# Encoder trunk on one core: weight parts kept in a DRAM scratch after their first split

## The chip, the cores and the metric

One NeuronCore of one Trainium2 chip runs the kernel; the other cores are idle. The metric is device time in microseconds (us) of one execution, as the median of several runs. Five engines matter here: PE (TensorE, matrix products), DVE (VectorE), ACT (ScalarE), POOL (GpSimd) and SP (SyncE), which computes nothing and issues every DMA of this kernel in the order of its own queue. An instruction waits on its engine until what it needs is there, and everything behind it on the same engine waits with it.

## The reference, cut to what matters

One layer and a final norm are applied to a prompt of 256 tokens and to a sample of 2048 tokens, with the same weights, all in float32:

```python
h = rms_norm(x, norm_mix_g)
proj = h @ w_in                       # 1024 x 1792: q, k, v, x_br, y_br
...
attn = bidir_gqa(apply_axial_rope(q, tables), apply_axial_rope(k, tables), v)
rec = recurrent_group(x_br, y_br, conv_w, conv_b, lru_wa, lru_ba, lru_wx, lru_bx, lru_lambda)
x = x + jnp.concatenate([attn, rec], axis=-1) @ w_out      # 1024 x 1024
h = rms_norm(x, norm_mlp_g)
x = x + jnp.square(jax.nn.relu(h @ w_up)) @ w_down         # 1024 x 4096, 4096 x 1024
return rms_norm(x, norm_final_g)
```

## The kernel before

Activations lie feature-major: 128 features on the partitions, up to 512 tokens (`NT`) on the free axis. TensorE multiplies a rounded form of float32 (float32r), so every operand is split into a high part (the value rounded) and a low part (the value minus the high part), and each product takes three matrix instructions: high weights by high tokens (L185), high weights by low tokens (L186), low weights by high tokens (L187). An instruction here takes a 128x128 weight block and 256 or 512 tokens.

The weights come as half tiles of 128x512, four 128x128 blocks each, and `WStream` (L128 to L169) streams them. For half tile i it loads the float32 values into a buffer `wf` (L145), writes the high part to a buffer `wh` by a cast (L160), and the low part to a buffer `wl` by a subtraction (L163). There are three buffers of each kind (`WBUFS`). When half tile `now` comes into use, `advance(now)` emits what is missing of the loads up to `now + 3` and of the casts and subtractions up to `now + 2` (`AHEAD = [4, 3, 3]`). The buffer of `wh` or `wl` for half tile i is that of half tile i - 3, so it comes free only when PE has done with i - 3; the buffer of `wf` comes free when the subtraction of i - 3 is done. In phase 1 cast and subtraction run on DVE. In phase 2 the cast runs on ACT; the subtraction runs on DVE, except in the prompt's block, where two of three run on POOL (`gtt`).

Phase 1 is the input projection `w_in`, in 28 half tiles. The list of half tiles names each of them three times: for the prompt (256 tokens), for the first half of the sample (two tiles of 512 tokens) and for the second half. Each time it is loaded and split again. Beside the projections run coroutines, one step at each tick of the projection stream: norms, gelu, query and key norms with rotation (`do_qk`), the recurrent group's gates and scans (`lru_sample`), and the prompt's attention. Most of their work is on DVE, and their results go to DRAM through SP.

Phase 2 goes through five blocks of tokens: the prompt's block p (256 tokens), then s0 to s3 (512 tokens each). `mlp` runs the output projection (16 half tiles), then up and down projections in groups (`up_down`, 64 and 64 half tiles), so 144 half tiles in a block and 720 in all, and all five blocks load and split all 144. At a block's start `load_cat` loads four operands of 1 MB each. The sample's attention is interleaved as a coroutine: its units for block s0 run during block p, those for s1 during s0, and so on, so s3 has none beside it. During block p the backward scans of the recurrent group (`lru_back`) run too, with their loads from DRAM. The last block's last eight half tiles are used twice and have memory of their own (`ws.kept`).

The order in each engine's queue is not the order of the program text. A planner that simulates the kernel sets it, with the text's order as priority; so a load can stand in SP's queue as soon as the planner sees its buffer free, ahead of where the text has it.

Of the kernel before, what the change touches and what calls it, by code (L numbers as in the profile page):

```python
# [19 lines left out]
P = 128  # L20
# [8 lines left out]
G = 4  # L29
# [14 lines left out]
# columns of the packed per-feature vectors  # L44
# [11 lines left out]
class Ticks:  # L56
    """Coroutines that emit a step of their work at each tick of the tensor engine's main stream."""
# [19 lines left out]
def trunk(ctx, tc, xT, w_in, w_out, w_up, w_down, vecs, wa, wx, cos, sin, outT):  # L77
# [11 lines left out]
    def loadr(out, src):  # L89
        """loads parts that were split before"""  # L90
        load(f32(out), src)
# [25 lines left out]
    # scratch in DRAM  # L117
# [10 lines left out]
    class WStream:  # L128
        """A sequence of half weight tiles (four stationaries each), loaded and split ahead of use."""

        def __init__(self, pool, srcs, ahead, bufs, copy, sub):
            self.pool, self.srcs, self.ahead, self.copy, self.sub = pool, srcs, ahead, copy, sub
            self.bufs = dict(zip(("wf", "wh", "wl"), bufs))
            self.at = [0, 0, 0]
            self.f, self.h, self.l = {}, {}, {}
            self.kept = {}  # memory for those that are used twice
# [4 lines left out]
        def load(self, end):  # L141
            while self.at[0] < end:
                i = self.at[0]
                self.f[i] = self._tile("wf", F32, i)
                load(self.f[i], self.srcs[i])  # L145
                self.at[0] += 1

        def advance(self, now):
            """emits what is due when half tile `now` comes into use"""
            self.load(min(now + self.ahead[0], len(self.srcs)))  # L150
            for st, a in list(enumerate(self.ahead))[1:]:
                while self.at[st] < min(now + a, len(self.srcs)):
                    i = self.at[st]
                    if i in self.kept:
                        tile_ = self.kept[i][st - 1]
                    else:
                        tile_ = self._tile(("wh", "wl")[st - 1], FR, i)
                    if st == 1:
                        self.h[i] = tile_
                        self.copy(i)(self.h[i], self.f[i])  # L160
                    else:
                        self.l[i] = tile_
                        self.sub(i)(self.l[i], self.f.pop(i), f32(self.h[i]), op=ALU.subtract)  # L163
# [7 lines left out]
    def faster(g, every):  # L171
        """a coroutine with one more step each time that `every` ticks have passed"""
# [16 lines left out]
    def rsqrt_newton(ps, r, w, mul):  # L189
        """r = -2 / sqrt(ps + eps), ps a mean square in PSUM"""  # L190
# [5 lines left out]
    # chunks of w_in in the order of use, for the prompt and for two halves of the sample; then all others by blocks  # L196
    order_p = [6, 7, 8, 9, 10, 11, 12, 13, 0, 1, 2, 3, 4, 5]
    order_s, order_t = ORDER_S, ORDER_T
    srcs = [h for m in order_p + order_s + order_t for h in halves(w_in[m])]
    n1 = len(srcs)  # L200
    for _ in segs:
        for m in range(0, KC, 2):
            srcs += [w_out[m][:, 0:512], w_out[m + 1][:, 0:512], w_out[m][:, 512:1024], w_out[m + 1][:, 512:1024]]
        for step in up_down():
            if step[0] == "u":
                srcs += halves(w_up[step[1] * G + step[2]])
            else:
                srcs += halves(w_down[step[1], step[2]])
    nb = (len(srcs) - n1) // len(segs)
    wp = ctx.enter_context(tc.tile_pool(name="w", bufs=1))  # L210
    ws = WStream(wp, srcs, AHEAD, WBUFS, lambda i: nc.vector.tensor_copy if i < n1 else nc.scalar.copy,
# [15 lines left out]
    right = ctx.enter_context(ExitStack())  # pools on the other side of the memory  # L227
# [5 lines left out]
    def load_cat(r, t0, n, up):  # L233
        """the output projection's operands of block r"""
# [8 lines left out]
    # ------------------------------------------------------------------ phase 1  # L243
    with ExitStack() as c1:
# [23 lines left out]
        def norm1(xs, n):  # L268
            """normalizes a token tile in place, but for the gains; then norm1_split applies them and splits"""
# [50 lines left out]
        sets = [0, 1]  # free ones of the two that hold a normalized token tile  # L320

        # the prompt's tile first
# [11 lines left out]
        CUT = 1022  # the sample's LRU segments: the first half's projections give this many outputs  # L334
        cuts = [(0, NT), (NT, CUT - NT)] + [(CUT + 342 * i, 342) for i in range(3)]

        # LRU constants: per-channel decay rates -8 softplus(-lam)
# [9 lines left out]
        # log1p(e) = 2 atanh(z), z = e/(2+e) <= 1/3  # L347
# [13 lines left out]
        # gate biases, halved for the tanh form of the sigmoid  # L361
        hba = ctile([P, 16], "hba")
        ts(hba, vec[:, V_BA:V_BA + 16], 0.5, None, op0=ALU.mult)
        # query and key gains; the -1/2 of the inverse root and the queries' 1/8 folded in
# [4 lines left out]
        # final gains with the -1/2 of the inverse root folded in  # L369
        ts(gfin, vec[:, V_GFIN:V_GFIN + 8], -0.5, None, op0=ALU.mult)  # L370

        # block-diagonal gate weights of one 128-channel chunk
# [13 lines left out]
        def project(i, h, n):  # L386
            """chunk i of the order for one token tile"""
# [22 lines left out]
        def do_qk(q, g, n, m, pos, outs):  # L410
            """head-wise norm and rotation of n columns of queries or keys, in pieces of m positions"""
# [63 lines left out]
        def lru_gates(gates, xb, xc, gt, o, m, c):  # L475
            """convolution and the tanh forms of the four gates for one piece; xb holds 2 tokens before, 1 after"""
# [20 lines left out]
        convs = {}  # pieces of each generation of xb whose convolution is still to come  # L497

        def lru(pieces, groups, w, done, gen):
            """coefficients of both directions and the forward states.  # L500
            pieces: (xb, offset, length, chunk); groups: (offset, length, chunk, carry or None)
            sigmoid = (tanh + 1)/2; a = exp(rate r); sqrt(1 - a^2) = (1 + a) sqrt(tanh(-rate r / 2))"""
# [45 lines left out]
        def lru_sample(c, xb, hf, gen):  # L548
            """one chunk for one half of the sample"""
# [12 lines left out]
        def lru_out(pool, dst, ge, ab, ub, hf, init):  # L562
            """backward states in place of ub, then the gated sum, split and stored"""
# [682 lines left out]
```

## Time and profile before

| | us |
|---|---|
| median of 3 runs | 3244.76 |
| lowest and highest run | 3243.56, 3248.42 |
| span of the profiled execution, first to last instruction | 3244.3 |
| PE busy in the span | 3014.7 (93%) |
| DVE busy | 2572.9 (79%) |
| ACT busy | 1714.2 (53%) |
| POOL busy | 1610.5 (50%) |
| DMA engines, mean busy share | 37% |

PE is the busiest engine, but the mean hides stages that have different limits, so the profile is read by stage. By the trace, the prompt's projections end near 150 us, the sample's projections near 570 us, block p near 1145 us, s0 near 1760 us, s1 near 2330 us, s2 near 2810 us, and s3 ends the span. PE's busy time counts matmuls that overlap in the pipeline once.

### The profile page before, as it was taken

What the parts mean: (1) busy time and instruction counts of PE and PEld (TensorE: products, weight loads), DVE (VectorE), ACT (ScalarE), POOL (GpSimd) and SP (SyncE); (2) the same over time, 40 slices, a digit from 0 to 9 for tenths busy, and PEclk for the clock granted to TensorE, in tenths of its full rate; (3) what the DMA queues carried; (4) which work ended last, traced back from release to release, by engine and by line L of the source; (5) the groups of instructions that cost most, each with busy time, mean ns of one, the idle gap of its engine ahead of it and who ended that gap; (6) DMA issues with size and microseconds to landing.
All of it is one profiled execution on the core that took longest, in us unless ns stands there. A gap on an engine that the chain in (4) does not pass through costs nothing.

```text
span 3244.3 us, 41376 instructions
## 1 busy us (share of the span) xinstructions
PE 3014.7 (93%) x13646; PEld 2425.1 (75%) x13646; DVE 2572.9 (79%) x3242; ACT 1714.2 (53%) x2954; POOL 1610.5 (50%) x1116
## 2 busy tenths in 40 slices
PE   6699899777898999999999999999999999999998
PEld 5576677556787778888887788888777888778887
DVE  8989988699999898887889988888898644464446
ACT  5475567555666566555555555555466333343333
POOL 4436634587899864453558444444664211321104
PEclk8899999798999999999999999999999999999999
DMA  5335344876333432222234322222442233552333
GB/s 159 116 119 194 113 148 156 223 217 189 114 98 100 153 122 74 72 73 75 77 102 150 120 76 70 81 75 71 142 148 72 89 94 95 167 164 95 94 95 104
DMA packets 222582, 380.78 MB, mean 117 GB/s; under 512 B 30752, under 2 KB 59680, under 8 KB 222368
## 3 DMA queue, kind: packets, MB, share of 16 engines
q1 hardware_dynamic: 222368, 378.15, 36.8%
q8 instruction: 107, 1.75, 0.2%
q14 instruction: 107, 0.88, 0.1%
HBM read 308.84 MB, written 69.21 MB: 117 GB/s over the span
## 4 chain that ended last, share of the span: by engine, by line
PE 60%; DVE 8%; issue 2%; DMA 2%; POOL 1%; ACT 1%; DVEq 0%; SPq 0%; POOLq 0%; ACTq 0%
PE ps_d L186 7%; PE ps_d L185 7%; PE ps_u L187 7%; PE ps_u L186 7%; PE ps_d L187 7%; PE ps_u L185 7%; PE po L940 3%; PE s_mx L839 3%; PE po L939 3%; PE s_t L936 3%; PE s_t L935 3%; DVE pl L947 2%; DVE mx L840 1%; DVE wl L163 1%; PE ps_o L185 1%
## 5 line engine op out<-in xcount | busy, mean ns | idle before, releaser
L951 POOL TENSOR_TENSOR acc<-acc,pf 128x512 f32<-128x512 f32 x448 | 692.2, 1545 | 395.6 <-ACT pf L943 359.6
L160 ACT CAST wh<-wf 128x512 fp32r<-128x512 f32 x712 | 439.7, 618 | 809.2 <-PE ps_d L186 361.4
L163 DVE TENSOR_TENSOR wl<-wf,wh 128x512 fp32r<-128x512 f32 x700 | 612.1, 875 | 211.0 <-ACT wh L160 205.6
L947 DVE TENSOR_TENSOR pl<-pf,ph 128x512 fp32r<-128x512 f32 x512 | 612.2, 1206 | 51.5 <-ACT ph L945 48.1
L187 PE MATMUL ps_u<-h2h,wl 128*128 128x512 f32 (+1 forms) x1280 | 478.8, 375 | 3.2 <-DVE wl L163 3.1
L186 PE MATMUL ps_u<-h2l,wh 128*128 128x512 f32 (+1 forms) x1280 | 478.6, 374 | 1.3 <-DVE h2l L977 1.3
L185 PE MATMUL ps_u<-h2h,wh 128*128 128x512 f32 (+1 forms) x1280 | 478.1, 374 | 0.0
L995 POOL TENSOR_TENSOR rl<-rl 128x512 f32<-128x512 f32 (+1 forms) x160 | 180.9, 1131 | 587.5 <-ACT uh L994 578.0
L185 PE MATMUL ps_d<-uh,wh 128*128 128x512 f32 (+1 forms) x1248 | 463.2, 373 | 4.1 <-ACT wh L160 3.5
L187 PE MATMUL ps_d<-uh,wl 128*128 128x512 f32 (+1 forms) x1248 | 462.5, 373 | 3.4 <-POOL wl L163 2.1
L186 PE MATMUL ps_d<-ul,wh 128*128 128x512 f32 (+1 forms) x1248 | 463.5, 373 | 2.2 <-DVE ul L997 2.2
L943 ACT ACTIVATE pf<-s_t 128x512 f32<-128x512 f32 x512 | 301.0, 594 | 225.6 <-PE s_t L936 120.9
L840 DVE TENSOR_REDUCE mx<-s_mx 128x1 f32<-128x512 f32 x512 | 344.9, 680 | 56.1 <-PE s_mx L839 55.0
L945 ACT ACTIVATE ph<-pf 128x512 fp32r<-128x512 f32 x512 | 316.9, 631 | 11.9 <-PE po L939 3.4
L187 PEld LDWEIGHTS ps_u<-h2h,wl 128*128 128x128 f32 x1280 | 243.0, 190 | 53.2 <-DVE wl L163 4.3
L186 PEld LDWEIGHTS ps_u<-h2l,wh 128*128 128x128 f32 x1280 | 243.2, 190 | 51.9 <-DVE h2l L977 2.1
L185 PEld LDWEIGHTS ps_u<-h2h,wh 128*128 128x128 f32 x1280 | 243.4, 190 | 50.7 <-issue 0.5
L185 PEld LDWEIGHTS ps_d<-uh,wh 128*128 128x128 f32 x1248 | 236.2, 189 | 53.5 <-ACT wh L160 4.9
L1108 DVE TENSOR_TENSOR y<-y,ps_d 128x512 f32<-128x512 f32 (+1 forms) x272 | 169.7, 625 | 133.5 <-PE ps_d L187 133.2
L187 PEld LDWEIGHTS ps_d<-uh,wl 128*128 128x128 f32 x1248 | 236.1, 190 | 51.8 <-POOL wl L163 2.6
L186 PEld LDWEIGHTS ps_d<-ul,wh 128*128 128x128 f32 x1248 | 236.3, 189 | 51.4 <-DVE ul L997 3.9
L185 PE MATMUL ps_in<-hh,wh 128*128 128x512 f32 (+1 forms) x560 | 221.5, 398 | 37.6 <-DVE wh L160 8.5
(277 smaller groups left out, 5823.6 us busy)
## 6 DMA issues: line engine op xcount, KB each, us to landing
wf<-in_w_up_dram SPq DMA_DIRECT2D x320, 256.0 KB, 2.7
wf<-in_w_down_dram SPq DMA_DIRECT2D x320, 256.0 KB, 2.7
wf<-in_w_in_dram SPq DMA_DIRECT2D x84, 256.0 KB, 2.9
wf<-in_w_out_dram SPq DMA_DIRECT2D x80, 256.0 KB, 2.9
x<-in_xT_dram SPq DMA_DIRECT2D x32, 256.0 KB, 5.1
qd<-q_ds SPq DMA_DIRECT2D x64, 128.0 KB, 3.0
cat<-a_ds SPq DMA_DIRECT2D x8, 1024.0 KB, 7.4
cat<-r_ds SPq DMA_DIRECT2D x8, 1024.0 KB, 9.7
```

Of the source, the lines that this page charges most:

```text
L160: self.copy(i)(self.h[i], self.f[i])
L163: self.sub(i)(self.l[i], self.f.pop(i), f32(self.h[i]), op=ALU.subtract)
L185: mm(ps, wh, xh, start=first, stop=False)
L186: mm(ps, wh, xl, start=False, stop=False)
L187: mm(ps, wl, xh, start=False, stop=last)
L840: nc.vector.tensor_reduce(mx[:, i, b:b + 1], s[:, :w], axis=AX.X, op=ALU.max)
L943: act(pf, s, AF.Exp)
L945: act(ph, pf, AF.Copy)
L947: tt(pl, pf, f32(ph), op=ALU.subtract)
L951: gtt(acc, acc, pf, op=ALU.add)
L995: gtt(e[:, :n], e[:, :n], e[:, :n], op=ALU.mult)
L1108: tt(y[:, :n], y[:, :n], ps[:, :n], op=ALU.add)
```

## The change

The list of half tiles becomes a list of keys that name which piece of which weight each one is. The first time that a key occurs, the low part gets a DRAM scratch of 128x512, and for `w_in` the high part gets one too. At the first use load, cast and subtraction are as before, and each new part is stored to its scratch by a DMA on SP's queue. At a later use of a `w_in` half tile, nothing is loaded into `wf`, and both parts are loaded from the scratch into `wh` and `wl`. At a later use of a half tile of `w_out`, `w_up` or `w_down`, the float32 values are loaded and cast by ACT as before, and the low part is loaded from the scratch in place of the subtraction. Buffer counts and distances (`WBUFS`, `AHEAD`) stay. Lines that only lose a comment are left out:

```diff
-        def __init__(self, pool, srcs, ahead, bufs, copy, sub):
+        def __init__(self, pool, srcs, saved, ahead, bufs, copy, sub):
             self.pool, self.srcs, self.ahead, self.copy, self.sub = pool, srcs, ahead, copy, sub
+            self.saved = saved
...
                 i = self.at[0]
-                self.f[i] = self._tile("wf", F32, i)
-                load(self.f[i], self.srcs[i])
+                hi, _, first = self.saved[i]
+                if first or hi is None:
+                    self.f[i] = self._tile("wf", F32, i)
+                    load(self.f[i], self.srcs[i])
                 self.at[0] += 1
...
                         tile_ = self._tile(("wh", "wl")[st - 1], FR, i)
+                    hi, lo, first = self.saved[i]
                     if st == 1:
                         self.h[i] = tile_
-                        self.copy(i)(self.h[i], self.f[i])
+                        if i in self.f:
+                            self.copy(i)(tile_, self.f[i])
+                            if first and hi is not None:
+                                store(hi, f32(tile_))
+                        else:
+                            loadr(tile_, hi)
                     else:
                         self.l[i] = tile_
-                        self.sub(i)(self.l[i], self.f.pop(i), f32(self.h[i]), op=ALU.subtract)
+                        f = self.f.pop(i, None)
+                        if first:
+                            self.sub(i)(tile_, f, f32(self.h[i]), op=ALU.subtract)
+                            store(lo, f32(tile_))
+                        else:
+                            loadr(tile_, lo)
...
-    srcs = [h for m in order_p + order_s + order_t for h in halves(w_in[m])]
-    n1 = len(srcs)
+    keys = [("i", m, e) for m in order_p + order_s + order_t for e in range(2)]
+    n1 = len(keys)
     for _ in segs:
         for m in range(0, KC, 2):
...
+            keys += [("o", m + e, b) for b in range(2) for e in range(2)]
+        keys += [(step, e) for step in up_down() for e in range(2)]
+    srcs, saved, scratch = [], [], {}
+    for key in keys:
...
+        srcs.append(halves(w)[e])
+        first = key not in scratch
+        if first:
+            scratch[key] = [dtile([P, 512], f"w{t}_d{len(scratch)}") if t == "l" or key[0] == "i" else None
+                            for t in ("h", "l")]
+        saved.append((*scratch[key], first))
```

## Rows read from the trace of the kernel before

**Rows 1.** Busy time (instructions) by engine, granted clock, DMA share in chosen stretches.

```profile
core 0: us, PE busy (x) PEld busy (x) DVE busy (x) ACT busy (x) POOL busy (x), PEclk, DMA share, GB/s
0.00:150.00 150.00, 98.00 (x508) 80.77 (x508) 140.22 (x238) 75.85 (x143) 70.33 (x55) 0.86 0.42 130
150.00:562.00 412.00, 374.34 (x1551) 291.63 (x1552) 361.55 (x471) 259.66 (x384) 195.81 (x122) 0.95 0.45 150
562.00:1145.00 583.00, 488.25 (x2715) 409.36 (x2714) 543.41 (x620) 339.95 (x636) 478.25 (x331) 0.93 0.52 155
1145.00:1240.00 95.00, 89.67 (x377) 69.28 (x376) 90.46 (x107) 59.91 (x106) 59.04 (x39) 1.00 0.34 109
1240.00:1760.00 520.00, 517.87 (x2237) 416.55 (x2237) 438.50 (x538) 292.78 (x506) 269.08 (x182) 1.00 0.27 87
1760.00:1840.00 80.00, 74.39 (x312) 57.00 (x311) 79.20 (x93) 48.18 (x83) 50.87 (x33) 1.00 0.41 136
2330.00:2410.00 80.00, 70.40 (x284) 54.18 (x283) 73.90 (x76) 45.08 (x77) 59.99 (x37) 0.96 0.50 159
2800.00:2880.00 80.00, 72.90 (x296) 55.94 (x295) 52.84 (x60) 31.02 (x52) 39.05 (x27) 0.98 0.66 211
2880.00:3180.00 300.00, 300.00 (x1287) 241.74 (x1286) 122.70 (x185) 101.82 (x171) 39.72 (x35) 1.00 0.30 96
```

**Rows 2.** Instruction groups of the split: whole span, then 150 to 562 us.

```profile
L163 DVE TENSOR_TENSOR wl<-wf,wh 128x512 fp32r<-128x512 f32 x700 | 612.1, 875 | 211.0 <-ACT wh L160 205.6
...
L163 DVE TENSOR_TENSOR wl<-wf,wh 128x512 fp32r<-128x512 f32 x50 | 43.2, 867 | 1.2
L160 DVE CAST wh<-wf 128x512 fp32r<-128x512 f32 x49 | 39.8, 815 | 0.2
```

**Rows 3.** Waits, 150 to 562 us: engine, waited for, total us, times, longest us.

```profile
POOL qk L436 <- DVE qsw L435: 52.4, 13, 11.0
...
PEld ps_in L187 <- DVE wl L163: 9.8, 8, 2.1
...
PEld ps_in L185 <- ACT qk L179: 8.5, 3, 7.3
...
PEld ps_in L185 <- DVE wh L160: 7.0, 5, 2.5
```

**Rows 4.** Timeline of PE, 2810 to 2870 us: the instructions that waited, idle before in brackets.

```profile
2824.14 0.50 PE L185 MATMUL ps_o<-cat,wh 128*128 128x512 f32 x1 [3.47 <-DMA cat<-r_ds]
2850.80 0.50 PE L187 MATMUL ps_o<-cat,wl 128*128 128x512 f32 x1 [1.36 <-DVE wl L163]
```

**Rows 5.** DMA view (count, KB, us to landing): 150-562, 562-650 (two lines), 650-820, 2900-3150 us.

```profile
wf<-in_w_in_dram SPq DMA_DIRECT2D x48, 256.0 KB, 3.0
...
q1 hardware_dynamic: 10501, 18.58, 78.3%
wf<-in_w_out_dram SPq DMA_DIRECT2D x13, 256.0 KB, 5.9
...
wf<-in_w_up_dram SPq DMA_DIRECT2D x22, 256.0 KB, 4.6
...
wf<-in_w_up_dram SPq DMA_DIRECT2D x48, 256.0 KB, 2.6
```

**Rows 6.** Timeline near 3000 us: casts of three half tiles that follow each other.

```profile
2999.67 0.62 ACT L160 CAST wh<-wf 128x512 fp32r<-128x512 f32 x1 [2.18 <-PE ps_d L186]
...
3002.47 0.62 ACT L160 CAST wh<-wf 128x512 fp32r<-128x512 f32 x1 [2.18 <-PE ps_d L186]
```

**Rows 7.** Waits of SP's queue, 150 to 562 us: total us, times, longest.

```profile
SPq L145 <- DVE wl L163: 105.3, 34, 11.7
SPq L430 <- DVE qk L434: 27.3, 16, 10.8
SPq L451 <- ACT qh L448: 22.8, 12, 6.4
```

**Rows 8.** Timeline of SP near 343 us: start, time on SP, one load.

```profile
342.75 0.33 SPq L145 DMA_DIRECT2D wf<-in_w_in_dram  x1
```

More of the change, by code (lines that the diff above doesn't have):

```diff
@@ L198, in trunk @@
     order_s, order_t = ORDER_S, ORDER_T
-    srcs = [h for m in order_p + order_s + order_t for h in halves(w_in[m])]
-    n1 = len(srcs)
+    keys = [("i", m, e) for m in order_p + order_s + order_t for e in range(2)]
+    n1 = len(keys)
     for _ in segs:
         for m in range(0, KC, 2):
[L203 to L208, printed above, removed]
+            keys += [("o", m + e, b) for b in range(2) for e in range(2)]
+        keys += [(step, e) for step in up_down() for e in range(2)]
+    srcs, saved, scratch = [], [], {}
+    for key in keys:
+        if key[0] == "i":
+            w, e = w_in[key[1]], key[2]
+        elif key[0] == "o":
+            w, e = w_out[key[1]], key[2]
+        else:
+            (kind, g, f), e = key
+            w = w_up[g * G + f] if kind == "u" else w_down[g, f]
+        srcs.append(halves(w)[e])
[4 more added lines that the diff above has]
+        saved.append((*scratch[key], first))
     nb = (len(srcs) - n1) // len(segs)
     wp = ctx.enter_context(tc.tile_pool(name="w", bufs=1))
-    ws = WStream(wp, srcs, AHEAD, WBUFS, lambda i: nc.vector.tensor_copy if i < n1 else nc.scalar.copy,
+    ws = WStream(wp, srcs, saved, AHEAD, WBUFS, lambda i: nc.vector.tensor_copy if i < n1 else nc.scalar.copy,
                  lambda i: gtt if n1 <= i < n1 + nb and i % POOL_SUB else tt)
```

## The prediction

> **What bounds the kernel now.** I read the page's busy times first, then the same by stage, then who waits for whom inside the stages where TensorE has gaps, and last the DMA landings and SP's queue. The reader is to see in the stage table that the kernel has no single limit [rows 1]. In the long stretches of blocks s0 to s3 PE is busy 517.9 of 520 us and 300.0 of 300; two more such stretches, 1840 to 2330 and 2410 to 2800 us, look alike. There PE is the bound and nothing that DVE gives up can shorten them. PE's gaps lie elsewhere: 52 us in the prompt's part (0 to 150), 37.7 us in the sample's projections (150 to 562), 95 us in block p, and 5.3, 5.6, 9.6 and 7.1 us, together 27.6 us, in four short stretches around the starts of s0 to s3. DVE is busy 93% of the prompt's part, 88% of the sample's projections, 93% of block p, and 95%, 99% and 92% at the starts of s0, s1 and s2. So DVE stands in the way in front of PE just where PE has gaps; but two of those places, the prompt's part and block p, are first uses, which the change leaves on DVE.
>
> **What is removed.** Of the 84 half tiles of `w_in`, 56 are later uses: each drops a cast of 0.815 us and a subtraction of 0.867 us, 56 x 1.682 = 94 us of DVE, of which the rows show 83 us inside 150 to 562 us [rows 2]. DVE there would go from 361.6 to some 279 us of 412, from 88% to 68%. In phase 2, 4 x 144 = 576 subtractions go, about 500 us of DVE by the mean of 875 ns [rows 2]. Of these, nearly all lie in stretches where PE has no gap, and I cost them at nothing gained: the cover is PE itself, and it cannot go.
>
> **Gain in the sample's projections.** PE's weight loads wait there 9.8 us for the low part and 7.0 us for the high part on DVE, 16.8 us, and 8.5 us for an evacuation by ACT [rows 3]; ACT's and POOL's own queues stand behind DVE, as the 52.4 us of POOL waiting for one DVE step of the rotation show [rows 3]. I take the 16.8 us whole, since these instructions no longer exist, and half of the evacuations' 8.5: 21 us. The bounds are 0 (another wait ends last in the same place) and all 37.7.
>
> **What takes the place of the wait there.** Both parts now come by DMA into `wh` and `wl`, whose buffers come free only when PE has finished the half tile three before. Before, the DMA went into `wf` ahead of that point, and only cast and subtraction lay behind it. For the second half tile of each chunk the buffer comes free one half tile before the chunk's end and the part is wanted one half tile into the next chunk: two half-tile times. One takes 2.80 us (two casts in a row, each released by PE [rows 6]), so the lead is 5.6 us. A `wf` load lands 3.0 us after its issue in this stage [rows 5]. The change adds 56 transfers of 256 KB here (112 loads for 56), 14.7 MB to some 62 MB (150 GB/s over 412 us [rows 1]), so the DMA share goes from 0.45 to about 0.56. Landings grow with the share in the rows: 2.6 us at 0.30, 3.0 at 0.45, 5.9 at 0.78 [rows 1, 5]; between these I take 3.8. That leaves 1.8 us, less 0.33 us of SP for each issue [rows 8]. On the other side stands SP's order: the queue also holds loads and stores that wait for DVE and ACT, and the two longest entries are 50.1 us in 28 waits, 1.8 us each and up to 10.8 [rows 7]. A weight load behind such a wait is late by what the slack doesn't cover, and PE waits for it. There are 28 such half tiles. The low end is 0, the high end all 28 by 1.8 us, 50 us. I take 8 us, about one in six, nearer to the low end since the mean wait just equals the slack and since the waits on SP are mostly for DVE, which gets lighter. Net for this stage: -13 us.
>
> **The prompt's part and block p: stores added.** The 28 first uses of `w_in` add 56 stores, 18 us of SP's time over 150 us at 0.33 us each [rows 1, 8], and the next `wf` load stands behind a store that waits for its subtraction. The loads have a buffer to spare; I take +1 us, between 0 and 4. Block p adds 144 stores. In its first 88 us (562 to 650) the DMA engines are already 78.3% busy and 13 output-projection loads take 5.9 us to land [rows 5]. The 17 half tiles of that time store 4.5 MB beside 18.6: share 78.3% x 23.1 / 18.6 = 97%. The extra 19% of 88 us is 17 us of DMA time; if it all delays the loads, that is the cost, and if the gaps swallow it, 0. PE and DVE both have gaps there, so I take the middle, +8. Later in block p a load lands in 4.6 us [rows 5], while 583 us for 144 half tiles is 4.0 us each and a `wf` buffer is free about three half tiles ahead; the stores hide behind DVE, which is the bound. If that cover goes, loads wait for stores, ACT's queue (the exponentials) waits behind the cast, and DVE starves; I carry that in the range.
>
> **The starts of s0 to s3.** Of PE's 27.6 us some 7 are waits for the 1 MB operands, 3.47 us at s3's start [rows 4], which no subtraction causes (the subtraction's own wait there is 1.36 us). Of the rest I take half, -10 us, since DVE is full at three of the four starts [rows 1] and the subtraction is one of its steady loads; the bounds are 0 and 20. Against it, at each start a low-part load is issued behind 2 MB of operands that are wanted at the same time, and then two 256 KB loads per half tile run beside the rest. I take +1 us at each start, +4; at most +16 if four half tiles of each are late by 1 us.
>
> **The long stretches.** A low-part load has its buffer when PE leaves half tile i - 3, so a lead of 5.6 us or more, against 2.6 us to land at a share of 0.30 [rows 1, 5, 6]. The share would go to about 0.6 in s3, the landing to about 4. Cost 0, with some 1.5 us to spare; if SP holds the load for longer, see the second rival.
>
> **The sum.** -21 + 8 + 1 + 8 - 10 + 4 = -10 us. The profiled span is 3244.3 us, half a microsecond under the median, so nothing is scaled: 3244.8 - 10 = 3235 us.
>
> **First rival: a larger gain.** The freed DVE time empties all queues behind it, no load is late, and block p's stores fit: -37.7 + 1 - 20 = -57 us, 3188 us; with half of that in place of my smaller shares, 3215. For it: the 52.4 us of POOL behind DVE [rows 3]. Against it: DMA waits take part of the same gaps. Chance 0.15, over the stretch below 3215.
>
> **Second rival: slower, late weights behind SP.** The mechanism is SP's order: one queue in which a load now waits for PE and for everything ahead of it, in place of a load that ran ahead. It decides from the point where SP holds a load longer than the slack, 1.8 us in the projections. Price: 50 us there, 17 in block p, 16 at the starts, less the gains of 31, plus 1: +53 us, 3298 us; at half of those costs, +11, 3256. I place its middle at 3272. For it: landings of 5.9 us under load [rows 5] and SP waits up to 10.8 us [rows 7]. Against it: the lead is twice the landing in quiet stretches. The Trainium skill's page "DMA: Bandwidth & Descriptors", section "Latency and other measured facts", speaks for this rival: it gives the access latency of HBM as 0.2 us on average and 2 us at high load. By that figure a load in the projections lands at an estimated 4.8 us, the slack falls to 0.8, and the sum would be about +10, 3255 us. The trace agrees in direction, with 2.6 us in the quiet stretch and 5.9 in the busy one. Chance 0.25.
>
> **Third rival: no change.** The gaps of PE stay because DMA waits end where DVE waits ended, each about as long: 3245 us. For it: PE alone takes 93% of the span. Chance 0.20.
>
> **How the numbers follow.** A measurement of this kernel can tell about 0.2%, 6.5 us, from no change. The forecast, a gain of 7 to 30 us, gets 0.40 and the larger gain 0.15: faster 0.55. Within 0.2%: 0.20. Slower: 0.25. As both signs hold chances, the forecast's own range is 3215 to 3238. The 8-in-10 range reaches into both rivals, 3200 to 3270, and leaves out about 0.08 below and 0.10 above.
>
> **What would show it.** In the profile after: DVE near 70% in the sample's projections and PE's gap there near 25 us; no wait of PE on L163 past the first uses, but some on the DMAs into `wh` and `wl`; in block p's first 90 us a DMA share above 0.9; the long stretches unchanged to 1%; DVE far lower in s0 to s3 with no effect. I am wrong if PE's waits for low-part loads sum to more than 30 us, if block p gets longer by more than 17 us, or if PE's gap in the projections closes altogether.

## The result and the profile after

The changed kernel takes 3220.62 us (median of 4 runs), the kernel before 3246.59 us beside it: ratio 0.9920, 95% interval 0.9906 to 0.9934, about 26 us faster. The forecast was 3235 us, and the range 3200 to 3270 holds the time. The profiled execution has a span of 3212.4 us, 31.9 us under the profiled one of before; its run is the fastest of the four, so stage differences below are to be read to some microseconds only.

The head of the page of the kernel after:

```profile
span 3212.4 us, 41900 instructions
PE 3007.6 (94%) x13646; PEld 2426.9 (76%) x13646; DVE 2066.8 (64%) x2554; ACT 1717.7 (53%) x2956; POOL 1540.9 (48%) x1116
```

DVE has 688 instructions fewer, as forecast, and lost 506 us of busy time (2572.9 before), where the prediction's two sums make 94 + 500 = 594. Its mean of 875 ns holds the slow subtractions of block p: they took 1268 ns there on DVE and 840 ns in s0 to s3. The durations of DVE's instructions fell by 573 us in sum; busy time counts neighbours that overlap once. The kernel got 26 us faster. The stage table of the kernel after, in the columns of [rows 1], with stretches near the matching stages:

```profile
core 0: us, PE busy (x) PEld busy (x) DVE busy (x) ACT busy (x) POOL busy (x), PEclk, DMA share, GB/s
0.00:130.00 130.00, 79.57 (x409) 69.07 (x410) 108.85 (x186) 62.08 (x122) 62.56 (x50) 0.76 0.70 232
130.00:555.00 425.00, 391.87 (x1651) 306.27 (x1650) 324.40 (x412) 274.30 (x409) 197.84 (x128) 0.98 0.58 190
555.00:1148.00 593.00, 496.20 (x2721) 410.64 (x2720) 536.70 (x613) 341.09 (x637) 471.49 (x333) 0.93 0.69 220
1148.00:1240.00 92.00, 90.39 (x390) 72.19 (x389) 77.68 (x88) 61.74 (x107) 54.02 (x37) 1.00 0.56 177
1240.00:1755.00 515.00, 515.00 (x2235) 415.14 (x2233) 348.12 (x414) 292.35 (x508) 256.14 (x185) 1.00 0.47 152
1755.00:1835.00 80.00, 80.00 (x347) 63.74 (x346) 67.05 (x82) 52.16 (x89) 47.10 (x33) 1.00 0.65 206
...
2310.00:2390.00 80.00, 77.97 (x333) 61.09 (x332) 63.06 (x71) 49.64 (x85) 58.58 (x39) 1.00 0.74 237
...
2775.00:2855.00 80.00, 73.64 (x301) 57.17 (x300) 28.63 (x38) 31.37 (x52) 30.81 (x24) 0.98 0.87 287
2855.00:3150.00 295.00, 295.00 (x1266) 237.66 (x1265) 48.99 (x72) 100.42 (x168) 38.21 (x35) 1.00 0.59 190
```

Against [rows 1], DVE falls from 88% to 76% in the sample's projections and from 95%, 99% and 92% to 84%, 84% and 79% at the starts of s0 to s2, where PE's gaps shrink from 5.3, 5.6 and 9.6 us to 1.6, 0 and 2.0. At the start of s3 the gap is 6.4 us (7.1 before). Block p's DVE share stays above 90%.

To see where the time went, I read the start of each stage's first half tile from PE's timeline, by counting the matmuls of the weight stream (24 per prompt chunk, 48 per sample chunk, 12 per half tile). The differences of these starts are the stage lengths, in us of the profiled executions; the tail is in s3. "Projections" is everything up to block p's first matmul. By this count three stage ends that stand ahead of the prediction are off. In the kernel before, the sample's first chunk starts at 99.6 us, so the prompt's projections end there and not near 150; s0 and s1 start at 1107 and 1726 us, and not near 1145 and 1760. The first stretch of [rows 1] therefore holds 50 us of the sample, and its stretches "at the starts" of s0 and s1 begin 38 and 34 us into these blocks. All kernels of the experiments stand in the same table:

| kernel | projections | p | s0 | s1 | s2 | s3 | s0 to s3 | ratio to before (95%) |
|---|---|---|---|---|---|---|---|---|
| before | 577.8 | 529.5 | 619.2 | 606.6 | 478.1 | 433.2 | 2137.1 | 1 |
| after | 570.4 | 539.5 | 611.9 | 592.4 | 468.5 | 429.7 | 2102.5 | 0.9920 (0.9906 to 0.9934) |
| p1_only | 573.3 | 529.1 | 617.1 | 606.3 | 476.4 | 429.8 | 2129.7 | 0.9973 (0.9964 to 0.9981) |
| p2_only | 579.5 | 542.1 | 611.3 | 592.4 | 465.6 | 431.8 | 2101.2 | 0.9935 (0.9923 to 0.9947) |
| dummy_sub | 570.3 | 540.8 | 616.4 | 607.1 | 482.1 | 434.1 | 2139.7 | 1.0029 (1.0018 to 1.0039) |
| no_lo_load | 571.5 | 527.0 | 612.0 | 592.7 | 467.1 | 422.9 | 2094.7 | 0.9851 (0.9837 to 0.9866) |
| p_stores_only | 571.5 | 540.0 | 619.5 | 607.9 | 478.7 | 430.8 | 2136.9 | 1.0025 (1.0012 to 1.0037) |
| p_stores_half | 572.8 | 536.0 | 617.8 | 604.0 | 480.3 | 430.4 | 2132.6 | 0.9993 (0.9983 to 1.0002) |
| pool_store | 574.8 | 667.3 | 612.6 | 592.8 | 465.9 | 430.1 | 2101.4 | 1.0303 (1.0282 to 1.0324) |
| prompt_plain | 584.4 | 541.2 | 613.5 | 592.9 | 470.8 | 433.0 | 2110.3 | 0.9960 (0.9948 to 0.9972) |
| wl4 | 574.1 | 541.7 | 610.4 | 592.9 | 464.4 | 426.5 | 2094.2 | 0.9903 (0.9888 to 0.9917) |
| wf4 | 568.0 | 533.3 | 611.9 | 592.4 | 470.6 | 432.4 | 2107.3 | 0.9887 (0.9872 to 0.9902) |
| save_in_s0 | 574.5 | 528.0 | 618.5 | 596.3 | 466.7 | 431.3 | 2112.8 | 0.9912 (0.9896 to 0.9929) |
| s0_wl4 | 574.3 | 530.0 | 617.1 | 597.6 | 465.3 | 429.3 | 2109.3 | 0.9935 (0.9922 to 0.9949) |

Four builds do the same work in s0 to s3 as the kernel before (before, p1_only, p_stores_only, p_stores_half), and they spread from 2129.7 to 2137.1 us there; four do the same as the kernel after (after, p2_only, pool_store, prompt_plain), from 2101.2 to 2110.3. Eight builds have the projections of the kernel after with the same buffers: 570.3 to 574.8. So a stage difference of up to 9 us over s0 to s3, or of 4.5 us in the projections, is within what another build of the planner's order or another execution gives.

In the two profiled executions the projections gained 7.4 us, block p lost 10.0, and s0 to s3 gained 34.6. Taken as means over the builds that do the same work in a stage, the change gives 6 us in the projections, costs 12 in block p (five builds with the stores, four without) and gives 30 over s0 to s3, 24 in all, near the 26 of the medians.

### The profile page after: what moved, and what is told of

The parts are those of the page before. It is cut to its first block, busy times and chain, and to the rows that moved or that the text cites. A ratio compares the mean times of both kernels' runs of the same rounds, so it can differ in the third digit from the quotient of the medians.

```text
span 3212.4 us, 41900 instructions
## 1 busy us (share of the span) xinstructions
PE 3007.6 (94%) x13646; PEld 2426.9 (76%) x13646; DVE 2066.8 (64%) x2554; ACT 1717.7 (53%) x2956; POOL 1540.9 (48%) x1116
## 4 chain that ended last, share of the span: by engine, by line
PE 64%; DVE 9%; DMA 5%; issue 3%; POOL 3%; ACT 2%; SPq 1%; DVEq 0%; POOLq 0%; ACTq 0%
PE ps_u L204 8%; PE ps_u L202 8%; PE ps_u L203 8%; PE ps_d L204 7%; PE ps_d L203 7%; PE ps_d L202 7%; PE s_t L964 3%; PE s_mx L867 3%; PE s_t L963 3%; PE po L968 3%; PE po L967 3%; DVE pl L975 2%; POOL acc L979 1%; DVE mx L868 1%; PE ps_o L202 1%
## 5 line engine op out<-in xcount | busy, mean ns | idle before, releaser
L979 POOL TENSOR_TENSOR acc<-acc,pf 128x512 f32<-128x512 f32 x448 | 653.3, 1458 | 421.5 <-ACT pf L971 405.3
L1025 DVE TENSOR_TENSOR ul<-rl,uh 128x512 fp32r<-128x512 f32 (+1 forms) x160 | 140.2, 876 | 333.0 <-POOL rl L1023 332.8
```

What stands on the lines that cost most here:

```text
L979: gtt(acc, acc, pf, op=ALU.add)
L1025: tt(ul[:, f, :n], e[:, :n], f32(uh[:, f, :n]), op=ALU.subtract)
```

## The experiments

The kernels below write the choice of the change as one function. For the n-th use of a key it says what is done with the high and with the low part: "plain" (split, not stored), "save" (split and store) or "load" (from the scratch). The changed kernel is

```python
def modes(key, n):
    if key[0] == "i":
        return ("load", "load") if n else ("save", "save")
    return "plain", "load" if n else "save"
```

**Each half of the change alone.** p1_only:

```diff
-    return "plain", "load" if n else "save"
+    return "plain", "plain"
```

> Only the w_in parts are kept in the scratch; the later blocks of phase 2 split again as before, and block p stores nothing. Theory: by the start times of the half tiles, the change is 7.4 us ahead when the projections end (570.4 against 577.8 us), and nothing after that differs from before, so the time is about 7 us under before. Rival (block p is bound by DVE and swallows what phase 1 brings): block p ends where it ended before, 1107 us, and the time is within 3 us of before.

Measured: 3237.91 us against 3244.52, ratio 0.9973, 6.6 us faster. The projections end 4.5 us ahead and block p keeps that (529.1 us). This is as the theory had it, and the rival falls: block p does not swallow the head start.

p2_only:

```diff
-        return ("load", "load") if n else ("save", "save")
+        return "plain", "plain"
```

> Only the low parts of w_out, w_up and w_down are kept; w_in is split at all three uses as before. Theory: block p pays about 10 us for its 144 stores, s0 to s3 gain 32 us as in the profile after (2.7 us behind at the start of s0, 29.6 us ahead at the last half tiles), so 20 to 24 us under before. Rival (the gain in s0 to s3 needs the head start or the other order from phase 1): less than 12 us under before.

Measured: 3224.62 us, ratio 0.9935, 19.9 us faster, just under the 20 of the theory. Block p pays 12.6 us and s0 to s3 give back 35.9. The two halves add: 6.6 + 19.9 = 26.5, and the whole change gives 26.

**Is the gain in s0 to s3 DVE's time?** dummy_sub does the subtraction again at each later use in phase 2, into a tile that nobody reads:

```diff
                         if lmode == "load":
                             loadr(tile_, lo)
+                            if f is not None:
+                                tt(self._tile("dm", FR, i), f, f32(self.h[i]), op=ALU.subtract)
```

> As the changed kernel, but at each later use in s0 to s3 DVE also does the subtraction into a tile that nobody reads; the low part still comes by DMA. Theory (the gain in s0 to s3 is DVE time given back at the blocks' starts): the gain of 32 us there goes, and with block p's 10 us and phase 1's 7 us the time is within 8 us of before. Rival (the gain is that PE's low part no longer stands behind ACT's cast and DVE's subtraction): the gain stays, 20 to 28 us under before.

Measured: 3252.93 us, 8.4 us over before, just past the 8 of the theory; s0 to s3 last 2139.7 us, as before. The whole gain is gone, though PE's low part stood behind no cast and no subtraction there. The stage table of dummy_sub at the four starts, columns as above:

```profile
1150.00:1242.00 92.00, 88.19 (x373) 68.85 (x373) 90.36 (x107) 59.90 (x107) 61.23 (x39) 1.00 0.50 165
1760.00:1840.00 80.00, 75.63 (x319) 58.46 (x318) 77.59 (x90) 48.10 (x83) 53.38 (x35) 1.00 0.61 195
2330.00:2410.00 80.00, 72.75 (x289) 56.17 (x289) 69.39 (x76) 44.93 (x76) 58.26 (x37) 0.94 0.67 210
2805.00:2885.00 80.00, 72.63 (x293) 55.82 (x292) 49.59 (x60) 30.97 (x50) 36.23 (x26) 0.96 0.84 276
```

With DVE back at 98%, 97% and 87%, PE issues 373, 319, 289 and 293 matmuls there, almost the 377, 312, 284 and 296 of [rows 1] (the 377 in 95 us, not 92), against 390, 347, 333 and 301 in the kernel after. By the start times of the half tiles, the first 32 of each block last 540.3 us over the four blocks in the kernel before, 514.5 after, and 540.2 in dummy_sub. So what the change gives in s0 to s3 is that the subtraction no longer runs, not that PE's low part comes sooner. The dummy subtraction also holds its `wf` buffer and slows POOL's additions again (last section); the run doesn't part these from DVE's time.

**What the stores and loads take back.** no_lo_load leaves them out in phase 2:

```diff
-    return "plain", "load" if n else "save"
+    return "plain", "load" if n else "plain"
...
+                    if st == 2 and lmode == "load" and lo is None:
+                        self.l[i] = self.h[i]
+                        self.f.pop(i)
+                        self.at[st] += 1
+                        continue
```

> As the changed kernel in phase 1; in phase 2 block p splits and stores nothing, and s0 to s3 neither subtract nor load a low part: the third product of each block of weights takes the high part again, so the low part's product is left out there. It gives the gain without the price of stores and loads. Theory (stores cost block p 10 us, loads cost the starts 4 us or less): 10 to 14 us faster than the changed kernel, 36 to 42 us under before. Rival (late low-part loads cost much at the blocks' starts): 50 us or more under before.

Measured: 3196.23 us, ratio 0.9851, 48.3 us under before, between the two expectations. Block p is back at 527.0 us, and s0 to s3 last 2094.7 us, 7.8 under the changed kernel, of which 6.8 in s3. Its stage table at the start of s3:

```profile
2765.00:2845.00 80.00, 78.36 (x330) 61.36 (x329) 29.17 (x39) 34.80 (x59) 30.86 (x25) 1.00 0.66 211
```

330 matmuls against 301 in the changed kernel: at s3's start, where no attention fills PE and the DMA share is 0.87 with the loads and 0.66 without, the loads cost about 29 x 0.23 = 7 us (300 us for 1287 matmuls in [rows 1] are 0.23 us each). At the other starts they cost nothing that shows.

**Block p's stores by themselves.** p_stores_only keeps the stores, and s0 to s3 split again:

```diff
-    return "plain", "load" if n else "save"
+    return "plain", "plain" if n else "save"
```

> As the changed kernel up to block p's end, with its 144 stores of low parts, but s0 to s3 load and subtract as before, so nobody reads the stored low parts. It gives the price of the stores alone. Block p lasts 529 us with the phase-1 part alone (first half tile of block p to first of s0) and 539.5 us in the changed kernel. Theory: the stores are the cause, block p lasts 538 to 542 us, s0 to s3 as before, so 2 to 7 us over before. Rival (block p is longer because its last loads already belong to s0, not because of stores): block p below 533 us and about 7 us under before.

Measured: block p 540.0 us, 3250.85 us, ratio 1.0025. The 144 stores alone lengthen block p by 11 us over p1_only.

p_stores_half stores half the columns:

```diff
-                                store(lo, f32(tile_))
+                                store(lo[:, :256], f32(tile_[:, :256])) if i >= n1 else store(lo, f32(tile_))
```

> As the one with stores and no later loads, but each store of block p takes only the first 256 of the 512 columns: half the bytes, the same number of DMAs, the same waits in SP's order. Half of each low part is not saved there, and nobody reads it. Theory of my prediction (the stores cost DMA bandwidth): the price halves, block p lasts 533 to 536 us. Rival (SP's order: a store waits for its subtraction and holds the loads behind it): block p stays at 538 to 542 us.

Measured: block p 536.0 us, at the upper edge of what bandwidth would give; 4 of the 11 us go with half the bytes. The time, ratio 0.9993, is 0.3% under that with full stores. So bytes count, but they are not all of it.

pool_store takes the stores out of SP's order:

```diff
-                                store(lo, f32(tile_))
+                                (nc.gpsimd.dma_start if i >= n1 else store)(lo, f32(tile_))
```

> The changed kernel with block p's 144 stores issued from POOL's queue and not from SP's; bytes are the same. If SP's order makes the stores dear, block p comes back to 529 to 533 us and the time is 32 to 36 us under before. If it is bandwidth, block p stays at 538 us or more and the time is 22 to 28 us under before. A third outcome: POOL, busy 80% of block p, pays for issuing, and block p passes 545 us.

Measured: 3344.64 us, ratio 1.0303; block p 667.3 us. It is the third outcome, far beyond its size. Groups of POOL in pool_store, 570 to 1200 us (instructions | busy us, mean ns | idle before):

```profile
L179 POOL DMA_DIRECT2D wl_d<-wl x143 | 78.8, 554 | 55.7 <-DVE wl L177 49.3 <-DMA k<-k_ds 3.6 <-issue 2.5
```

Each issue holds POOL for 554 ns, and 49.3 us POOL stands still because a store waits for a subtraction on DVE, with the attention's sums queued behind it. So this run says nothing on SP's order; it shows what a waiting store does to the engine that issues it.

wf4 gives the float32 loads a fourth buffer and one half tile more lead:

```diff
-AHEAD = [4, 3, 3]
-WBUFS = [3, 3, 3]
+AHEAD = [5, 3, 3]
+WBUFS = [4, 3, 3]
```

> The changed kernel with a fourth buffer for the float32 values and their loads emitted one half tile earlier. Block p lasts 539.5 us in the changed kernel, 529 without stores. Theory (the stores make the float32 loads late, and ACT's cast waits for them): block p lasts 530 to 535 us, 30 to 35 us under before. Rival (the stores cost bandwidth that the other loads of block p miss, or delay the subtraction itself): block p 537 us or more, 22 to 28 us under before.

Measured: 3207.74 us, ratio 0.9887, 36.2 us under before; block p 533.3 us. In block p (570 to 1108 us) ACT's casts waited for float32 loads; the kernel after first:

```profile
ACT wh L168 <- DMA wf<-in_w_down_dram: 24.1, 15, 4.3
ACT wh L168 <- DMA wf<-in_w_up_dram: 13.9, 13, 3.2
ACT wh L168 <- DMA wf<-in_w_out_dram: 8.6, 3, 4.3
```

The same waits in wf4:

```profile
ACT wh L170 <- DMA wf<-in_w_out_dram: 15.2, 5, 4.1
ACT wh L170 <- DMA wf<-in_w_up_dram: 3.9, 3, 2.3
ACT wh L170 <- DMA wf<-in_w_down_dram: 2.9, 3, 1.7
```

For the up and down weights 38.0 us of waits became 6.8, and 6.2 of the 11 us of block p came back: block p is as the theory had it. But the kernel before has such waits too, without any store (570 to 1108 us):

```profile
ACT wh L160 <- DMA wf<-in_w_down_dram: 22.1, 10, 3.8
ACT wh L160 <- DMA wf<-in_w_out_dram: 16.9, 7, 3.2
ACT wh L160 <- DMA wf<-in_w_up_dram: 2.2, 4, 1.2
```

For the up and down weights that is 24.3 us. So the fourth buffer also takes away waits that the stores did not cause, and no run gives that buffer to a kernel without stores. That more lead for the float32 loads takes back 6 us is shown; that late loads make up half of the stores' price is not.

DVE's busy time tells more of where the price arises. It is nearly the same in all these kernels, so block p's length goes with DVE's idle time. The first 90 us of block p and the rest of it, before, after, and the rest in wf4, columns as above:

```profile
577.80:667.80 90.00, 65.96 (x336) 54.99 (x335) 66.78 (x70) 46.56 (x83) 55.51 (x38) 0.83 0.85 228
667.80:1107.30 439.50, 375.30 (x2186) 317.38 (x2186) 432.15 (x497) 263.42 (x502) 387.80 (x271) 0.95 0.46 138
```

```profile
570.40:660.40 90.00, 65.51 (x315) 52.10 (x314) 66.06 (x72) 49.18 (x88) 57.77 (x37) 0.80 0.89 269
660.40:1109.90 449.50, 383.35 (x2212) 320.90 (x2212) 428.93 (x495) 261.45 (x499) 376.46 (x270) 0.95 0.66 212
```

```profile
658.00:1101.30 443.30, 379.08 (x2195) 315.54 (x2194) 431.67 (x496) 263.64 (x498) 382.75 (x270) 0.95 0.67 212
```

In the first 90 us DVE is idle 23.2 us before and 23.9 after. In the rest it is idle 7.4 us before, 20.6 after and 11.6 in wf4: block p's price arises there.

**Where the stores stand.** prompt_plain saves the `w_in` parts one use later:

```diff
-        return ("load", "load") if n else ("save", "save")
+        return (("plain",) * 2, ("save",) * 2, ("load",) * 2)[n]
```

> The changed kernel with the parts of w_in saved one use later: the prompt's 28 half tiles are split and not stored, the sample's first half splits and stores, only its second half loads. The prompt's part was 28 to 30 us late in the changed kernel and had caught up to 5 us by the fourth chunk of the sample. Theory (the delay ends in a wait that was there anyway, and later relief is what counts): no delay in the prompt, but half the relief, so block p starts at 573 to 575 us, 20 to 24 us under before. Rival (the lost 28 us are paid for in part): block p starts at 566 us or earlier, 30 us or more under before.

Measured: 3231.53 us, ratio 0.9960. Both expectations miss: the projections end at 584.4 us, 6.7 us later than before, in an execution that is the slowest of its seven, 6 us over their median. The prompt's delay is gone (its last chunk starts at 92.2 us against 124.3 in the changed kernel), and by the fifth sample chunk the two are level (193.9 and 193.4). The run doesn't show that the delay is free, since it also splits and stores where the changed kernel loads.

The relief in the sample's second half gives nothing in either kernel. The two halves of the sample, from the first chunk of each to the first of the next, before and after:

```profile
99.60:353.20 253.60, 210.18 (x821) 158.45 (x821) 227.57 (x292) 132.52 (x200) 130.87 (x83) 0.91 0.43 141
353.20:577.80 224.60, 206.63 (x880) 163.53 (x879) 198.39 (x262) 147.25 (x220) 99.19 (x62) 0.96 0.43 142
```

```profile
129.20:345.50 216.30, 197.97 (x817) 153.13 (x817) 172.04 (x217) 130.48 (x195) 109.87 (x70) 0.98 0.61 200
345.50:570.40 224.90, 206.00 (x879) 162.86 (x880) 166.90 (x211) 150.57 (x226) 97.19 (x63) 0.97 0.53 174
```

The second half lasts 224.6 and 224.9 us, though DVE gives up 31 us of work in it; in prompt_plain it lasts 228.3. In the kernel before PE's weight loads waited for the split some 3 us there, against 13.7 from the third chunk (153.8 us) to the end of the first half. So all that the change gives in the projections comes from the first half, which prompt_plain splits as before and stores besides: from the second chunk to the second half it takes 219.8 us, against 218.7 in the kernel before and 203.1 after.

save_in_s0 does the same for phase 2:

```diff
-    return "plain", "load" if n else "save"
+    return "plain", ("plain", "save", "load")[min(n, 2)]
```

> The low parts of phase 2 are saved one use later: block p splits and stores nothing, s0 splits on DVE and stores, s1 to s3 load. Block p's price of 10 to 12 us goes, and s0's gain of 7 us goes with it. Theory: s0's DMA engines are busy only 0.27 to 0.34 of the time before, so its 144 stores cost 3 us or less, s0 lasts 617 to 623 us (619.2 before), block p 528 to 531, and the time is 24 to 32 us under before, as the changed kernel. Rival (stores cost wherever DVE is full, by the wait of the next subtraction for its buffer): s0 lasts 627 us or more, 20 us under before or less.

Measured: 3215.85 us, ratio 0.9912, 28.1 us under before. Block p 528.0 and s0 618.5 us are as the theory had them: in s0 the 144 stores cost nothing that shows. The whole comes out as the changed kernel does (0.9920): block p's price is gone, and so is a use of the gain.

**More lead for the low parts.** wl4:

```diff
-AHEAD = [4, 3, 3]
-WBUFS = [3, 3, 3]
+AHEAD = [4, 3, 4]
+WBUFS = [3, 3, 4]
...
+                    if st == 2 and lmode != "load" and i >= self.at[1]:
+                        break
```

> The changed kernel with a fourth buffer for low parts, and low-part loads emitted one half tile earlier (2.8 us more lead). In s0 to s3 the changed kernel gains 32 us and the one with neither subtraction nor load 40 us, so the loads cost 8 us there. Theory (they are late at the blocks' starts because a load has two half-tile times of lead behind 2 MB of operands): most of the 8 us comes back, 4 to 8 us under the changed kernel, 30 to 36 us under before. Rival (the loads take bandwidth from the 1 MB operands, and lead changes nothing): within 3 us of the changed kernel.

Measured: 3213.32 us, ratio 0.9903, 30.6 us under before, at the edge of the theory. s0 to s3 last 2094.2 us, as without any load, while projections and block p are 3.7 and 2.2 us longer than in the changed kernel. Waits of PE's weight loads on DMAs, 1110 to 3190 us, in the kernel after:

```profile
PEld ps_o L202 <- DMA cat<-r_ds: 4.9, 2, 3.7
PEld ps_u L204 <- DMA wl<-wl_d: 4.7, 3, 2.1
PEld ps_d L204 <- DMA wl<-wl_d: 1.0, 1, 1.0
```

and in wl4:

```profile
PEld ps_o L203 <- DMA cat<-r_ds: 2.7, 2, 2.5
PEld ps_u L205 <- DMA wl<-wl_d: 1.9, 2, 1.7
```

s0_wl4 joins the last two.

> Both findings together: low parts of phase 2 saved in s0 (block p without stores) and a fourth buffer for low parts. If the parts add, with the stages of the runs before: projections end at 574 us, block p 528, s0 617, s1 593, s2 464, s3 427, together 3203 us of span, 38 to 43 us under before and below every kernel so far. Rival (the fourth buffer helped s0 to s3 only by shifting work from block p, whose 542 us it had): block p 535 us or more, 30 us under before or less.

Measured: 3220.02 us, ratio 0.9935, a miss. Block p (530.0 us) is as expected, but s0 to s3 last 2109.3 us, only 3.5 under save_in_s0, where 8 were expected. So the fourth buffer's 8 us in wl4 are not shown to be its effect; they are within the spread of builds. wf4 has the lowest ratio of the kernels that compute everything; its interval overlaps that of wl4.

## Why the prediction was right, and where its terms were not

The direction, the mechanism and the stages were right: DVE was in the way where PE had gaps; most of its 506 us gave nothing; block p paid for stores. The size was not: -10 us forecast, -26 measured; the wide range holds it, and the forecast's own band, a gain of 7 to 30 us, does too. Term by term, in the profiled executions:

**The starts of s0 to s3: -10 + 4 forecast, -34.6 measured over s0 to s3 (some 30 as a mean over builds).** This is the term that was mis-sized. The prediction took PE's gaps as length less busy time, 27.6 us at the four starts, and half of the rest after the operands' waits. Busy time hides slow matmuls: those that follow each other more slowly still count as busy. The counts in [rows 1] show it. The quiet stretch issues 1287 matmuls in 300 us, 4.29 per us. The four starts issue 377 + 312 + 284 + 296 = 1269 in 335 us, where 4.29 would give 1437: 168 too few, 39 us, and not 27.6. (Some instructions have a smaller weight block or fewer columns, so this is an estimate.) A part of what busy time hides is the granted clock, 0.96 and 0.98 of full speed at the starts of s2 and s3 in [rows 1]. After, it is 390 + 347 + 333 + 301 = 1371 in 332 us, 53 too few, 12 us. So 27 us came back at the starts alone, against the 20 that I had called the most, and the first 32 half tiles of the blocks give 25.8 by their start times; the other 8 or 9 lie behind them, within the spread of builds. dummy_sub shows that it is the subtraction that was in the way. The loads' +4 was half of the 7.8 us of no_lo_load, with its place wrong: at s3's start alone, not at each.

**The sample's projections: -21 + 8 forecast, -7.4 measured with the prompt.** From the sample's first chunk to block p, DVE's busy time fell by 87 us, near the 94 forecast, from 89% to 77% of the stretch; the forecast 68% came from a stretch that began two chunks later. The waits on cast and subtraction are gone, all 16.8 us. The waits of PE's weight loads in the kernel after, 130 to 555 us, the view that the prediction read, show what came in their place:

```profile
PEld ps_in L202 <- ACT qk L196: 10.6, 3, 5.3
PEld ps_in L202 <- DMA wh<-wh_d: 6.2, 4, 2.7
PEld ps_in L204 <- DMA wl<-wl_d: 2.8, 5, 1.1
```

The loads are late by 6.2 + 2.8 = 9.0 us, where I had 8: that term was right. The evacuation, of whose 8.5 us I gave half away, waits 10.6. So the rows sum to 16.8 - 9.0 - 2.1 = 5.7 us, near what was measured (an estimate, since waits need not add up to time); the term that was too large is the evacuation's. I had also taken the stretch as one, and its second half gave nothing. The landings were 3.2 us for high and 3.6 for low parts:

```profile
wl<-wl_d SPq DMA_DIRECT2D x54, 256.0 KB, 3.6
wh<-wh_d SPq DMA_DIRECT2D x53, 256.0 KB, 3.2
```

I had interpolated 3.8. The estimate of 4.8 us that I had worked out from the Trainium skill ("DMA: Bandwidth & Descriptors", "Latency and other measured facts") is not borne out at a share of 0.58. The second rival needed weight loads that come late again and again; PE waited for them nine times in this stretch.

**The prompt: +1 forecast, +29.6 at its end, some 5 left at the sample's fifth chunk.** The reason given, a buffer to spare, was wrong. PE's weight loads wait 12.8 us for casts in the first 130 us now, and the DMA share of the first 100 us is 0.76 against 0.50. But the sample's first chunk takes two token tiles, and the second tile's normalized tokens come when they came before. Their low parts, before and after:

```profile
L303 DVE SCALAR_TENSOR_TENSOR hl<-x,vec,hh x8: 737/741/1762, 125.0 to 135.6; 128x512 fp32r<-128x512 f32 x8
```

```profile
L331 DVE SCALAR_TENSOR_TENSOR hl<-x,vec,hh x8: 744/747/750, 128.6 to 133.9; 128x512 fp32r<-128x512 f32 x8
```

The last of the eight starts at 135.6 and at 133.9 us. So the sample's second chunk starts 7.9 us later than before (142.4 against 134.5), the fifth 4.9 us later, and the second half 7.7 us earlier. That the cost is small was luck: it came out for a reason that the prediction did not see. No run shows that it is nothing.

**Block p: +8 forecast, +10.0 measured (12 as a mean over builds).** The size is right, the place is not, so the size is luck in part. I had put all of it into the first 88 us as DMA time, at a share of 97%. From 555 to 650 us the share is 79.7%:

```profile
q1 hardware_dynamic: 12970, 23.04, 79.7%
wl_d<-wl SPq DMA_DIRECT2D x16, 256.0 KB, 4.9
wf<-in_w_out_dram SPq DMA_DIRECT2D x13, 256.0 KB, 5.2
```

The first of these lines is the queue's packets, MB and share, the others issues with KB and us to landing. The loads land no later than before (5.9 us in [rows 5]), and 23.04 MB in 95 us take about the share that 18.58 MB in 88 us took: I had raised the share with the bytes. DVE stands idle no longer in the first 90 us than before. The price came later in the block, where I had called the stores hidden behind DVE: DVE is idle 13 us more there, ACT's casts wait 38.0 us for the up and down weights against 24.3, and one more `wf` buffer takes back 6 us. "If that cover goes, loads wait for stores" named this, as a risk and not as the case.

**The long stretches: 0 forecast.** Right: between 1240 and 1755 us PE was and is at the bound, with DVE down from 84% to 68%.

**What stays open.** How block p's price divides between bytes and SP's order; what a fourth `wf` buffer gives without stores; whether a fourth low-part buffer helps s0 to s3; and what bounds the second half of the sample's projections, where freed DVE time gave nothing.

## What to carry to other kernels

Work taken off an engine pays only where the bound engine has gaps behind it, and there it is worth more than the gaps in busy time say: compare instructions issued per microsecond with a quiet stretch, not idle time. Look at what each new store holds back in its queue: with one buffer more for the loads behind it, 6 of 11 us came back here. Moving the stores to a stretch with room took their price away, but cost one use of what they save, and the total stayed the same. A delay can end in a wait that was there anyway, as most of the prompt's 30 us did, so follow a slip to where it ends before paying to remove it.

## What the runs showed of the hardware

POOL's own additions became faster when DVE's subtractions went. The additions of the attention's sums in s0, the kernel before (1240 to 1760 us) and after (1240 to 1755 us):

```profile
L951 POOL TENSOR_TENSOR acc<-acc,pf 128x512 f32<-128x512 f32 x120 | 182.5, 1520 | 150.3 <-ACT pf L943 133.0 <-DVE wl L163 15.3
```

```profile
L979 POOL TENSOR_TENSOR acc<-acc,pf 128x512 f32<-128x512 f32 x122 | 170.5, 1397 | 164.1 <-ACT pf L971 162.9
```

1520 ns fell to 1397 for the same instruction, and the 15.3 us of POOL's waits that end with the subtraction are gone. In dummy_sub, where DVE subtracts again, it takes 1503 ns (1240 to 1760 us). The Trainium skill's page "SBUF — State Buffer", section "Who interferes with whom", says that a VectorE instruction with two SBUF inputs contends with a GpSimd instruction that reads SBUF; these rows agree.

A transfer of 256 KB landed hardly later when the mean DMA share doubled: in s3's long stretch the float32 loads took 2.6 us at a share of 0.30 [rows 1, 5], and in the kernel after, at 0.59 (2855 to 3150 us):

```profile
wl<-wl_d SPq DMA_DIRECT2D x106, 256.0 KB, 2.7
wf<-in_w_down_dram SPq DMA_DIRECT2D x53, 256.0 KB, 2.9
```

The prediction had read a growth with the mean share out of three stages, 4 us at 0.6. The mean share alone does not set the landing: at 0.58 in the projections it was 3.2 and 3.6 us. That the slow landings belong to bursts, as the 4.9 and 5.2 us at 79.7% above, is likely but not shown.
